# Half of W1's columns by seven block products for eight in a two-layer decoder trunk, with the weight sums made between the steps of the preceding round's W2 product

## The chip, the core and the metric

The kernel runs on one core of a Trainium2 chip. The core has a matrix engine (TensorE, in the profile PE, its weight loads PEld), a vector engine (DVE), a scalar engine (ACT), GpSimd (POOL) and a queue engine that issues the loads (SP). The metric is the device time of one execution in microseconds (us). The kernel before takes 2276.84 us, the median of three runs (2275.48 to 2276.86).

## What is computed

Two layers of a decoder trunk, on 256 rows of 2048 columns in float32. Only the last line of a layer is touched by the change:

```python
x = x + mixed @ w_out[layer]
h2 = _rms(x, norm2_g[layer])
x = x + jnp.square(jax.nn.relu(h2 @ mlp_w1[layer])) @ mlp_w2[layer]
```

W1 is 2048 x 8192, W2 is 8192 x 2048. The four mixers before W_out stay as they are.

## The kernel before, in words

**Precision.** Every large product is made from float32 numbers split into a high and a low part: `x = xh + xl`, `w = wh + wl`, and three products, `xl wh + xh wh + xh wl`, are summed in PSUM. The activations are the stationary operand, transposed to "slots" of two 128-row k tiles by 256 rows (names `Ah`, `Al` for the normed residual, `Bh`, `Bl` for the hidden layer). The weights are the moving operand.

**Weights.** A chunk is two k tiles by 512 columns, 128 x 1024 or 512 KB. `raw` (L138) issues its load on SP's queue into one of four `raw` buffers. `split_chunk` (L147) makes `wh` by a copy on ACT (L153; three buffers) and `wl = raw - wh` by a subtraction on DVE (L154; two buffers). A `raw` buffer is free when both have read it, a `wl` buffer when TensorE has used it.

**A product** (`product`, L157) of 2048 by 512 is eight chunks of 12 matmuls of 128x512: eight on `wh` (L172, L173), then four on `wl` (L177), over two row tiles. It sums into two of four PSUM banks with the tag `mm`; four more banks (tag `ms`) serve the transposes.

**The MLP** (in `run`) goes in four rounds of 2048 hidden columns. In a round, four products of W1, each followed by relu on ACT (L987), the square on DVE (L988), eight transposes and the split into slots `B` (`to_slots`, L195); then four products of W2, each added to the residual `x` on DVE (`residual`, L934). Before it, the last four W_out products each write four transposed k tiles of the residual, times the gain, to slots `A` (`split_slot` with gain, L217 and L218).

**Order.** A scheduler with its own timeline puts each engine's instructions into one fixed order; operations under `hp` (high priority) are placed ahead. On each engine, the instructions then run in that order. SP's loads too.

Of the kernel before, what the change touches and what calls it, by code (L numbers as in the profile page):

```python
# [12 lines left out]
F32 = mybir.dt.float32  # L13
F32R = mybir.dt.float32r
I32 = mybir.dt.int32
AF = mybir.ActivationFunctionType
# [4 lines left out]
P = 128  # L21
# [33 lines left out]
class Trunk:  # L55
# [18 lines left out]
    # ---------------------------------------------------------------- helpers  # L74
# [62 lines left out]
    # ------------------------------------------------------- weights and products  # L137
# [19 lines left out]
    def product(self, chunks, lhs, n=512, before=None):  # L157
        """sum over k of lhs[k]^T @ w[k]; chunks hold two k each. Returns the PSUM tiles of both row tiles."""
# [19 lines left out]
        return acc  # L178
# [16 lines left out]
    def to_slots(self, src, cols, slots, j0, gain=None):  # L195
        """src(t): token-major [128, >=cols] tiles; transposes cols into slot pairs from j0 on."""
        nc = self.nc
        for jj in range(cols // 256):
            pt = self.misc("tp").rearrange("p (k s) -> p k s", k=2)
# [6 lines left out]
            self.split_slot(pt, slots[j0 + jj], gain, 2 * (j0 + jj))  # L206
# [154 lines left out]
    # ---------------------------------------------------------------- norm of the residual  # L361
# [32 lines left out]
    def evac_normed(self, acc, heads, d, r, tag):  # L394
        """token-major copies times r, normed per head"""
# [25 lines left out]
    def head_tr(self, src, dst, engine):  # L421
        """src(t): token-major [128, 4 * 128]; dst [128, 2, 4, 128] (row tile, head, row)"""
# [29 lines left out]
    def s5_table(self, i):  # L452
        """[128, 2, 256]: cos and sin of t * theta for the state column i."""
# [120 lines left out]
    def vones(self, acc, r, name):  # L574
        """values with a column of ones per head: [128, 2, 4, 129]"""
# [50 lines left out]
    # ---------------------------------------------------------------- native sparse attention  # L626
# [8 lines left out]
    def nsa_kv(self, acc, kcol, r, tag):  # L635
        """the key and value column blocks times r, and 128 ** -0.5 times what norms the keys, [128, 2]"""
# [21 lines left out]
    def rope1_tr(self, k, tag):  # L658
        """[128 rows, 128] x 2 -> roped and transposed [128, 256]"""
# [10 lines left out]
    def nsa_compress(self, layer, kcT, vcT):  # L670
        """k_cmp^T [128, 15], its norm scale [15, 1], and [v_cmp | 1] [15, 129]"""
# [5 lines left out]
        for w, xT in enumerate((kcT, vcT)):  # L677
# [6 lines left out]
            # four lags at a time: each column tile sums its own, the rest of its rows stay zero  # L684
# [89 lines left out]
    # ---------------------------------------------------------------- retention  # L774
# [8 lines left out]
    def ret(self, qT, kT, v):  # L783
        """normed retention output, token-major"""
# [150 lines left out]

    def run(self):
# [16 lines left out]
        for layer in range(self.depth):  # L953
# [9 lines left out]
            h2 = self.slots("A")  # L963
            early, late = kt[8:], kt[:8]
            for n in range(4):
                self.residual(self.product([ins["w_out"][layer, 0, n, c] for c in range(4)], early), n)
            for n in range(4):
                self.residual(self.product([ins["w_out"][layer, 1, n, c] for c in range(4)], late), n)
                with self.hp():
                    self.to_slots(lambda t: self.x[t][:, n * 512:], 512, h2, 2 * n, self.gains[:, 1, layer])  # L970
                    self.sumsq(ss, n)
            with self.hp():
                r = self.rstd(ss, "b")
            kt2 = self.ktiles(h2)
# [3 lines left out]
            hT = None  # L978
            for rd in range(4):
                hid = self.slots("B")  # L980
                for n in range(4):
                    acc = self.product([ins["w1"][layer, 4 * rd + n, c] for c in range(8)], kt2)
                    hs = []
                    with self.hp():
                        for t in range(NT):
                            h = self.wk.tile([P, 512], F32, name="hid", tag="rp", bufs=3)
                            nc.scalar.activation(h, acc[t], AF.Relu, scale=r[:, t:t + 1])  # L987
                            V.tensor_tensor(h, h, h, ALU.mult)  # L988
                            hs.append(h)
                        self.to_slots(lambda t: hs[t], 512, hid, 2 * n)  # L990
                kh = self.ktiles(hid)
                if rd == 3 and not last:
                    hT = self.slots("A")
                for n in range(4):
                    acc = self.product([ins["w2"][layer, rd, n, c] for c in range(8)], kh)
                    self.residual(acc, n)
                    if rd == 3:
                        if last:
                            for t in range(NT):
                                nc.scalar.dma_start(self.out[t * P:(t + 1) * P, n * 512:(n + 1) * 512],  # L1000
                                                    self.x[t][:, n * 512:(n + 1) * 512])
                        else:
                            with self.hp():
                                self.to_slots(lambda t: self.x[t][:, n * 512:], 512, hT, 2 * n,
                                              self.gains[:, 0, layer + 1])
                                self.sumsq(ss, n)
# [10 lines left out]
def _chunks(w):  # L1017
    """[K, N] -> [K/256, 128, 2, N]: partition rows of two k tiles side by side"""
# [4 lines left out]
def _layout(i):  # L1023
# [23 lines left out]
    # state columns: partition = (group of the pair, state), column = pair  # L1047
# [44 lines left out]
```

## Time and profile before

| what | value |
|---|---|
| median of three runs | 2276.84 us |
| span of the profiled execution (no other time of it is listed) | 2274.8 us |
| TensorE busy | 2249.3 us (99%) |
| DVE busy | 1411.6 us (62%) |
| ACT busy | 1083.1 us (48%) |
| loaded from memory | 405.61 MB, 179 GB/s over the span |
| granted TensorE clock | 0.999 of full speed |

The profiled execution's span is 2.0 us under the median of the runs. "Busy" of an engine is the time in which one of its instructions ran; matmuls overlap each other in the records (one lasts 0.39 us and the next begins 0.23 us after it), so the count of matmuls in a time says more than their durations. "Idle before" names what ended an engine's idle time. The MLP of layer 0 lies between about 440 and 1135 us from the span's start, that of layer 1 between about 1500 us and the end.

### The profile page before, as it was taken

What the parts mean: (1) busy time and instruction counts of PE and PEld (TensorE: products, weight loads), DVE (VectorE), ACT (ScalarE), POOL (GpSimd) and SP (SyncE); (2) the same over time, 40 slices, a digit from 0 to 9 for tenths busy, and PEclk for the clock granted to TensorE, in tenths of its full rate; (3) what the DMA queues carried; (4) which work ended last, traced back from release to release, by engine and by line L of the source; (5) the groups of instructions that cost most, each with busy time, mean ns of one, the idle gap of its engine ahead of it and who ended that gap; (6) DMA issues with size and microseconds to landing.
All of it is one profiled execution on the core that took longest, in us unless ns stands there. A gap on an engine that the chain in (4) does not pass through costs nothing.

```text
span 2274.8 us, 29209 instructions
## 1 busy us (share of the span) xinstructions
PE 2249.3 (99%) x10732; PEld 1831.1 (80%) x10732; DVE 1411.6 (62%) x2105; ACT 1083.1 (48%) x1410; POOL 144.7 (6%) x396
## 2 busy tenths in 40 slices
PE   8999999999999999999999999999999999999999
PEld 7777778888888888888877777888888888888887
DVE  8988975555555555455569997566554554555554
ACT  6456554544344344344545664445444443443443
POOL 0213111000000000000002212010000000000000
PEclk9999999999999999999999999999999999999999
DMA  7544735555655555555554456355555556556554
GB/s 252 165 133 130 241 113 167 183 182 191 194 185 192 190 192 185 195 186 185 186 175 155 131 152 206 120 178 183 186 192 189 190 181 201 187 190 191 191 194 167
DMA packets 115919, 409.62 MB, mean 180 GB/s; under 512 B 14016, under 2 KB 14272, under 8 KB 115776
## 3 DMA queue, kind: packets, MB, share of 16 engines
q1 hardware_dynamic: 113184, 405.06, 53.8%
q10 hardware_dynamic: 2592, 2.70, 0.3%
q8 instruction: 84, 1.38, 0.2%
q14 instruction: 59, 0.48, 0.1%
HBM read 405.61 MB, written 2.10 MB: 179 GB/s over the span
## 4 chain that ended last, share of the span: by engine, by line
PE 86%; DVE 7%; POOL 3%; issue 2%; ACT 2%; DMA 1%; DVEq 0%; ACTq 0%; SPq 0%
PE mm L177 27%; PE mm L172 27%; PE mm L173 27%; DVE wl L154 2%; PE tp L203 2%; DVE w L515 1%; PE glu L551 1%; POOL rst L89 1%; PE bu L502 1%; PE nsc L759 0%; PE yp L530 0%; PE npv L769 0%; POOL rst L91 0%; POOL rst L90 0%; PE cmp L693 0%
## 5 line engine op out<-in xcount | busy, mean ns | idle before, releaser
L153 ACT ACTIVATE wh<-raw 128x1024 fp32r<-128x1024 f32 (+1 forms) x752 | 790.5, 1052 | 1055.0 <-PE mm L173 944.7
L154 DVE TENSOR_TENSOR wl<-raw,wh 128x1024 fp32r<-128x1024 f32 (+1 forms) x752 | 908.0, 1213 | 594.5 <-PE mm L177 557.6
L172 PE MATMUL mm<-wh,Al 128*128 128x512 f32 (+1 forms) x1728 | 670.1, 389 | 1.9 <-ACT wh L153 1.5
L173 PE MATMUL mm<-wh,Ah 128*128 128x512 f32 (+1 forms) x1728 | 669.1, 388 | 0.0
L172 PE MATMUL mm<-wh,Bl 128*128 128x512 f32 x1280 | 498.4, 389 | 0.9 <-DVE Bl L213 0.9
L173 PE MATMUL mm<-wh,Bh 128*128 128x512 f32 x1280 | 498.4, 389 | 0.0
L177 PE MATMUL mm<-wl,Ah 128*128 128x512 f32 (+1 forms) x1728 | 466.9, 391 | 10.9 <-DVE wl L154 10.5
L177 PEld LDWEIGHTS mm<-wl,Ah 128*128 128x128 f32 x1728 | 316.0, 188 | 88.4 <-DVE wl L154 18.4
L172 PEld LDWEIGHTS mm<-wh,Al 128*128 128x128 f32 x1728 | 325.1, 188 | 73.2 <-issue 4.6
L173 PEld LDWEIGHTS mm<-wh,Ah 128*128 128x128 f32 x1728 | 325.2, 188 | 69.7 <-issue 5.6
L177 PE MATMUL mm<-wl,Bh 128*128 128x512 f32 x1280 | 344.2, 391 | 0.2 <-DVE wl L154 0.2
L172 PEld LDWEIGHTS mm<-wh,Bl 128*128 128x128 f32 x1280 | 240.3, 188 | 51.1 <-DVE Bl L213 1.1
L173 PEld LDWEIGHTS mm<-wh,Bh 128*128 128x128 f32 x1280 | 240.3, 188 | 49.7
L177 PEld LDWEIGHTS mm<-wl,Bh 128*128 128x128 f32 x1280 | 238.6, 188 | 49.0 <-DVE wl L154 0.6
L934 DVE TENSOR_TENSOR x<-mm,x 128x512 f32<-128x512 f32 x96 | 61.8, 686 | 105.5 <-PE mm L177 105.5
L213 DVE TENSOR_TENSOR Bl<-tp,Bh 128x512 fp32r<-128x512 f32 x76 | 52.1, 687 | 70.9 <-ACT Bh L212 70.9
L86 POOL TENSOR_SCALAR rv<-rv 128x2 f32<-128x2 f32 x4 | 1.0, 244 | 879.8 <-DVE rv L372 879.8
L987 ACT ACTIVATE hid<-mm,rb 128x512 f32<-128x512 f32 x64 | 40.6, 685 | 24.2 <-PE mm L177 24.2
L212 ACT ACTIVATE Bh<-tp 128x512 fp32r<-128x512 f32 x76 | 40.8, 584 | 5.7 <-PE tp L203 5.7
L988 DVE TENSOR_TENSOR hid<-hid 128x512 f32<-128x512 f32 x64 | 41.2, 684 | 0.0
L515 DVE TENSOR_TENSOR_SCAN w<-mag,z 128x256 f32<-128x256 f32 x64 | 40.7, 678 | 0.0
L218 DVE SCALAR_TENSOR_TENSOR Al<-tp,gains,Ah 128x256 fp32r<-128x256 f32 x64 | 29.3, 478 | 16.9 <-ACT Ah L217 16.9
(300 smaller groups left out, 1187.4 us busy)
## 6 DMA issues: line engine op xcount, KB each, us to landing
raw<-in_w_dram SPq DMA_DIRECT2D x512, 512.0 KB, 3.4
raw<-in_w_main_dram SPq DMA_DIRECT2D x160, 512.0 KB, 4.0
raw<-in_w_out_dram SPq DMA_DIRECT2D x64, 512.0 KB, 3.6
aux<-in_wcmp_dram SPq DMA_DIRECT2D x16, 512.0 KB, 5.2
raw<-in_w_gate_dram SPq DMA_DIRECT2D x16, 268.0 KB, 2.6
x<-in_x_dram SPq DMA_DIRECT2D x8, 256.0 KB, 5.1
aux<-in_s5g_dram SPq DMA_DIRECT2D x4, 512.0 KB, 4.8
out_dram<-x ACTq DMA_DIRECT2D x8, 256.0 KB, 2.1
```

What stands on the lines that cost most here:

```text
L153: self.nc.scalar.activation(h[:, :cols], r[:, :cols], AF.Copy)
L154: self.nc.vector.tensor_tensor(l[:, :cols], r[:, :cols], h[:, :cols].bitcast(F32), ALU.subtract)
L172: nc.tensor.matmul(acc[t], rows(xl, t), mov(wh, j), start=k == 0, stop=False)
L173: nc.tensor.matmul(acc[t], rows(xh, t), mov(wh, j), start=False, stop=False)
L177: nc.tensor.matmul(acc[t], rows(lhs[k][0], t), mov(wl, j), start=False, stop=k == nk - 1)
L203: nc.tensor.transpose(pt[:, kk, t * P:(t + 1) * P], src(t)[:, c:c + P], self.ident)
L212: nc.scalar.activation(h, pt, AF.Copy)
L213: nc.vector.tensor_tensor(l, pt, h.bitcast(F32), ALU.subtract)
L515: V.tensor_tensor_scan(w[:, c, :], mg, z[:, c, :], 0.0, ALU.mult, ALU.add)
L934: self.nc.vector.tensor_tensor(x, acc[t], x, ALU.add)
L987: nc.scalar.activation(h, acc[t], AF.Relu, scale=r[:, t:t + 1])
L988: V.tensor_tensor(h, h, h, ALU.mult)
```

## The change

Two neighbouring column blocks of W1 (512 columns each, blocks 0 and 1 of a round) and the two row tiles and the two k tiles of a chunk form a 2 x 2 by 2 x 2 block product. The kernel before makes it by eight block products; the change makes it by seven (a Strassen-Winograd scheme), each again by three matmuls (`three`). Blocks 2 and 3 of a round are made as before (`plain`). For each chunk the seven are: two with unchanged operands (`first_steps`, banks p1, p2), and five with sums of blocks (`sums_steps`, banks p3 to p7).

- `sums_slot`: the sums of activation blocks, made once per layer when the slots `A` are written, with their own split (`Sh`, `Sl`).
- `sums_steps`: per chunk it loads both W1 blocks (block 0 a second time), makes four differences on DVE (L251 to L254; `t13`, `t24`), splits three operands on ACT (L262) and DVE (L263), and issues 15 matmuls.
- `pair_first`, `pair_last`: combine p1 to p7 to the four results; relu and square are now both on ACT (`act2`).
- `mlp`: in rounds 1 to 3 one sums step is put after every fourth chunk of the preceding round's W2 product (`second`); in round 0 after every second chunk of the two plain W1 products. The W2 product of the last round comes alone.

```diff
+    def sums_slot(self, pt, slot, gain, k):
...
+        a = self.wk.tile([P, 2, SEQ], F32, name="ga", tag="w")
+        for kk in range(2):
+            nc.scalar.activation(a[:, kk, :], pt[:, kk, :], AF.Copy, scale=gain[:, k + kk:k + kk + 1])
+        nc.scalar.activation(h, a, AF.Copy)
+        V.tensor_tensor(l, a, h.bitcast(F32), ALU.subtract)
...
+        V.tensor_tensor(s[:, 0, :], blk(1, 0), blk(1, 1), ALU.add)
+        V.tensor_tensor(s[:, 1, :], s[:, 0, :], blk(0, 0), ALU.subtract)
+        V.tensor_tensor(s[:, 2, :], blk(0, 0), blk(1, 0), ALU.subtract)
+        V.tensor_tensor(s[:, 3, :], blk(0, 1), s[:, 1, :], ALU.subtract)
...
+        nc.scalar.activation(sh, s, AF.Copy)
+        V.tensor_tensor(sl, s, sh.bitcast(F32), ALU.subtract)
...
+    def three(self, acc, x, w, first, last):
+        nc = self.nc
+        (xh, xl), (wh, wl) = x, w
+        nc.tensor.matmul(acc, xl, wh, start=first, stop=False)
+        nc.tensor.matmul(acc, xh, wh, start=False, stop=False)
+        nc.tensor.matmul(acc, xh, wl, start=False, stop=last)
...
+        for c, src in enumerate(chunks):
+            w = self.split_chunk(src)
+            for kk in range(2):
+                self.three(acc[kk], [x[:, kk, :P] for x in slots[c]], [y[:, kk * 512:(kk + 1) * 512] for y in w],
+                           c == 0, c == last)
...
+                b1 = self.raw(chunks1[c]).rearrange("p (k n) -> p k n", k=2)
+                b2 = self.raw(chunks2[c]).rearrange("p (k n) -> p k n", k=2)
+                ta, tb = (self.wk.tile([P, 2, 512], F32, name=nm, tag="aux", bufs=2) for nm in ("t13", "t24"))
+                V.tensor_tensor(ta[:, 0, :], b2[:, 0, :], b1[:, 0, :], ALU.subtract)
+                V.tensor_tensor(ta[:, 1, :], b2[:, 1, :], b2[:, 0, :], ALU.subtract)
+                V.tensor_tensor(tb[:, 0, :], b2[:, 1, :], ta[:, 0, :], ALU.subtract)
+                V.tensor_tensor(tb[:, 1, :], tb[:, 0, :], b1[:, 1, :], ALU.subtract)
...
+                ah = self.wp.tile([P, 1024], F32R, name="t13h", tag="wh", bufs=3)
+                al = self.wp.tile([P, 1024], F32R, name="t13l", tag="wl", bufs=2)
...
+                for h, l, x in ((bh, bl, b2[:, 1, :]), (ah, al, f2(ta)), (dh, dl, f2(tb))):
+                    nc.scalar.activation(h, x, AF.Copy)
+                    V.tensor_tensor(l, x, h.bitcast(F32), ALU.subtract)
...
+            self.three(acc[3], S(3), (bh, bl), *f)
+            self.three(acc[5], S(0), half((ah, al), 0), *f)
+            self.three(acc[7], S(2), half((ah, al), 1), *f)
+            self.three(acc[6], S(1), half((dh, dl), 0), *f)
+            self.three(acc[4], [x[:, 1, P:] for x in slots[c]], half((dh, dl), 1), *f)
...
+            if rd:
+                mix(second(rd - 1, hid), ys, 4, 1)
+                hid = self.slots("B")
+            else:
+                hid = self.slots("B")
+                mix(both(plain(rd, n, hid) for n in (2, 3)), ys, 2, 1)
+            done = pair_last(p, v1, c11)
...
-            for rd in range(4):
-                hid = self.slots("B")
-                for n in range(4):
-                    acc = self.product([ins["w1"][layer, 4 * rd + n, c] for c in range(8)], kt2)
```

**The order on DVE in a W2 product.** In the kernel before, DVE's rows of the W2 products of a round are (`x` the residual, `wl` the low parts of the weights):

```order
L934 TENSOR_TENSOR x_78<-mm_5031,x_78 128x512
L934 TENSOR_TENSOR x_79<-mm_5032,x_79 128x512
L154 TENSOR_TENSOR wl<-raw,wh 128x1024 x8
L934 TENSOR_TENSOR x_78<-mm_5179,x_78 128x512
L934 TENSOR_TENSOR x_79<-mm_5180,x_79 128x512
L154 TENSOR_TENSOR wl<-raw,wh 128x1024 x8
```

In the changed kernel, the rows of the second group of four chunks of such a product, with the step at the product's end (`t13l`, `t24l`, `bl` are low parts of the sums and of one block):

```order
L154 TENSOR_TENSOR wl<-raw,wh 128x1024 x2
L251 TENSOR_TENSOR t_6988<-raw 128x512
L252 TENSOR_TENSOR t_6988<-raw 128x512
L263 TENSOR_TENSOR bl<-raw,bh 128x512
L253 TENSOR_TENSOR t_6989<-raw,t_6988 128x512
L1033 TENSOR_TENSOR x_78<-mm_6719,x_78 128x512
L1033 TENSOR_TENSOR x_79<-mm_6720,x_79 128x512
L154 TENSOR_TENSOR wl<-raw,wh 128x1024
L254 TENSOR_TENSOR t_6989<-t_6989,raw 128x512
L263 TENSOR_TENSOR t13l<-t_6988,t13h 128x1024
L263 TENSOR_TENSOR t24l<-t_6989,t24h 128x1024
```

The two L251/L252 rows read two `raw` buffers and stand behind the split of the product's last chunk and of the next one's first; the two additions to `x` stand behind four of the step's rows.

**The order on DVE at the start of the MLP.** Before, from the last W_out product's addition to `x` on:

```order
L934 TENSOR_TENSOR x_78<-mm_4234,x_78 128x512
L934 TENSOR_TENSOR x_79<-mm_4235,x_79 128x512
L154 TENSOR_TENSOR wl<-raw,wh 128x1024 x2
L372 TENSOR_REDUCE rv<-ss 128x2
L218 SCALAR_TENSOR_TENSOR Al_3633<-tp,gains,Ah_3632 128x256
L154 TENSOR_TENSOR wl<-raw,wh 128x1024
L218 SCALAR_TENSOR_TENSOR Al_3635<-tp,gains,Ah_3634 128x256
```

and in the changed kernel (`ga`, `gs` the activations and their block sums, `Sl` the sums' low parts):

```order
L1033 TENSOR_TENSOR x_78<-mm_4294,x_78 128x512
L215 TENSOR_TENSOR Sl<-gs,Sh 128x512
L1033 TENSOR_TENSOR x_79<-mm_4295,x_79 128x512
L154 TENSOR_TENSOR wl<-raw,wh 128x1024 x2
L215 TENSOR_TENSOR Sl<-gs,Sh 128x512
L471 TENSOR_REDUCE rv<-ss 128x2
L209 TENSOR_TENSOR gs<-ga 128x128
L207 TENSOR_TENSOR gs<-ga 128x128
L154 TENSOR_TENSOR wl<-raw,wh 128x1024
L207 TENSOR_TENSOR gs<-ga 128x128
L209 TENSOR_TENSOR gs<-ga 128x128
L154 TENSOR_TENSOR wl<-raw,wh 128x1024
```

Each `wl` row there now has rows of the sums between it and the next.

## Rows read from the trace of the kernel before

**Rows 1.** The page, parts 1, 2 and 4: busy time, clock, chain that ended last.

```profile
PE 2249.3 (99%) x10732; PEld 1831.1 (80%) x10732; DVE 1411.6 (62%) x2105; ACT 1083.1 (48%) x1410; POOL 144.7 (6%) x396
...
PE 86%; DVE 7%; POOL 3%; issue 2%; ACT 2%; DMA 1%; DVEq 0%; ACTq 0%; SPq 0%
```

**Rows 2.** Stretches: us, length, busy (count) per engine, clock, DMA share, GB/s.

```profile
core 0: us, PE busy (x) PEld busy (x) DVE busy (x) ACT busy (x) POOL busy (x), PEclk, DMA share, GB/s
...
600.00:700.00 100.00, 100.00 (x455) 83.08 (x454) 51.20 (x50) 44.58 (x48) 0.00 (x0) 1.00 0.57 189
...
1200.00:1300.00 100.00, 96.34 (x492) 74.11 (x491) 92.73 (x174) 60.17 (x89) 21.89 (x45) 1.00 0.47 145
```

**Rows 3.** DVE's timeline in a W2 product: start, duration, idle time before.

```profile
599.05 1.23 DVE L154 TENSOR_TENSOR wl<-raw,wh 128x1024 fp32r<-128x1024 f32 x1 [1.50 <-PE mm L177]
601.77 1.22 DVE L154 TENSOR_TENSOR wl<-raw,wh 128x1024 fp32r<-128x1024 f32 x1 [1.49 <-PE mm L177]
604.49 1.23 DVE L154 TENSOR_TENSOR wl<-raw,wh 128x1024 fp32r<-128x1024 f32 x1 [1.50 <-PE mm L177]
...
610.78 1.29 DVE L934 TENSOR_TENSOR x<-mm,x 128x512 f32<-128x512 f32 x2 [2.35 <-PE mm L177]
611.98 2.35 DVE L154 TENSOR_TENSOR wl<-raw,wh 128x1024 fp32r<-128x1024 f32 x2
```

**Rows 4.** Groups by shape: busy us, mean ns of one, idle before.

```profile
L154 DVE TENSOR_TENSOR wl<-raw,wh 128x1024 fp32r<-128x1024 f32 x736 | 896.4, 1223 | 593.6 <-PE mm L177 556.7 <-issue 29.0 <-ACT np L761 4.4
...
L988 DVE TENSOR_TENSOR hid<-hid 128x512 f32<-128x512 f32 x64 | 41.2, 684 | 0.0
...
L388 DVE TENSOR_TENSOR k1r<-ko,rc 128x128 f32<-128x128 f32 x8 | 2.2, 278 | 0.0
```

**Rows 5.** The same view for ACT.

```profile
L153 ACT ACTIVATE wh<-raw 128x1024 fp32r<-128x1024 f32 x736 | 780.1, 1060 | 1045.2 <-PE mm L173 938.6 <-DVE wl L154 29.4 <-DMA raw<-in_w_main_dram 19.3
L212 ACT ACTIVATE Bh<-tp 128x512 fp32r<-128x512 f32 x76 | 40.8, 584 | 5.7 <-PE tp L203 5.7
```

**Rows 6.** Waits of TensorE, 0 to 440 us, costliest: total us, times, longest.

```profile
PE mm L177 <- DVE wl L154: 4.2, 7, 1.8
```

**Rows 7.** SP's own waits: total us, times, longest.

```profile
SPq L140 <- DVE wl L154: 1806.7, 700, 11.5
```

**Rows 8.** The tile raw, 500 to 1000 us: loads, and their time to landing.

```profile
L140 SPq DMA_DIRECT2D raw<-in_w_dram x180: 327/328/328, 501.7 to 997.7; - x180
...
DMA to landing us min/median/max: 3.0/3.4/5.7
```

**Rows 9.** The tile raw, 0 to 30 us, where loads crowd.

```profile
L140 SPq DMA_DIRECT2D raw<-in_w_main_dram x11: 327/328/559, 1.7 to 29.1; - x11
...
DMA to landing us min/median/max: 3.7/5.6/8.8
```

**Rows 10.** The page, part 2: GB/s in the first slices of 57 us.

```profile
GB/s 252 165 133 130 241 113 167 183 182 191 194 185 192 190 192 185 195 186 185 186 175 155 131 152 206 120 178 183 186 192 189 190 181 201 187 190 191 191 194 167
```

**Rows 11.** TensorE's timeline, transposes of a hidden tile, 461 us.

```profile
461.04 1.04 PE L203 MATMUL tp<-ident,hid 128*128 128x128 f32 x8
...
461.83 1.17 PE L177 MATMUL mm<-wl,Ah 128*128 128x512 f32 x4
```

More of the change, by code (lines that the diff above doesn't have):

```diff
@@ L157, in product, with product_steps @@
     def product(self, chunks, lhs, n=512, before=None):
+        acc = []
+        for _ in self.product_steps(acc, chunks, lhs, n, before):
+            pass
+        return acc
+    def product_steps(self, out, chunks, lhs, n=512, before=None):
         nc = self.nc
@@ new lines, in three, with first_steps @@
+    def three(self, acc, x, w, first, last):
+        nc = self.nc
+        (xh, xl), (wh, wl) = x, w
+        nc.tensor.matmul(acc, xl, wh, start=first, stop=False)
+        nc.tensor.matmul(acc, xh, wh, start=False, stop=False)
+        nc.tensor.matmul(acc, xh, wl, start=False, stop=last)
+    def first_steps(self, out, chunks, slots):
+        acc = [self.ps.tile([P, 512], F32, name=f"p{i}", tag="mm") for i in (1, 2)]
+        last = len(chunks) - 1
+        for c, src in enumerate(chunks):
[3 more added lines that the diff above has]
+                           c == 0, c == last)
+            if c == last:
+                out.extend(acc)
+            yield
@@ L193, in ktiles, with to_slots @@
         return [(slots[k // 2][0][:, k % 2, :], slots[k // 2][1][:, k % 2, :]) for k in range(KT)]
-    def to_slots(self, src, cols, slots, j0, gain=None):
+    def to_slots(self, src, cols, slots, j0, gain=None, sums=None, bank=None):
         nc = self.nc
         for jj in range(cols // 256):
-            pt = self.misc("tp").rearrange("p (k s) -> p k s", k=2)
+            pt = (bank or self.misc)("tp").rearrange("p (k s) -> p k s", k=2)
             for kk in range(2):
@@ L205, in to_slots @@
                 slots[j0 + jj] = self.slot("B", j0 + jj)
-            self.split_slot(pt, slots[j0 + jj], gain, 2 * (j0 + jj))
+            if sums is not None:
+                sums.append(self.sums_slot(pt, slots[j0 + jj], gain, 2 * (j0 + jj)))
+            else:
+                self.split_slot(pt, slots[j0 + jj], gain, 2 * (j0 + jj))
     def split_slot(self, pt, slot, gain=None, k=0):
@@ L934, in residual, with act2, mlp, mix @@
                 self.nc.vector.tensor_tensor(x, acc[t], x, ALU.add)
+    def act2(self, c, x, r, t):
+        S = self.nc.scalar
+        S.activation(c, x, AF.Relu, scale=r[:, t:t + 1])
+        S.activation(c, c, AF.Square)
+    def mlp(self, layer, h2, sums, r, ss, last):
+        nc = self.nc
+        V = nc.vector
+        kt2 = self.ktiles(h2)
+        w1 = lambda rd, n: [self.ins["w1"][layer, 4 * rd + n, c] for c in range(8)]
+        bank = lambda name: self.ps.tile([P, 512], F32, name=name, tag="mm")
+        tmp = lambda nm, tag, n: self.wk.tile([P, 512], F32, name=nm, tag=tag, bufs=n)
+        nxt = [None]
+        def mix(xs, ys, every, off):
+            for i, _ in enumerate(xs):
+                if i % every == off:
+                    next(ys, None)
+            for _ in ys:
+                pass
+        def pair_first(rd):
+            p = []
+            for _ in self.first_steps(p, w1(rd, 0), h2):
+                pass
+            with self.hp():
+                v1, c11 = tmp("v1", "ev", 4), tmp("c11", "ev", 4)
+                nc.scalar.activation(v1, p[0], AF.Copy)
+                V.tensor_tensor(c11, p[1], v1, ALU.add)
+                self.act2(c11, c11, r, 0)
+            return v1, c11
+        def pair_last(p, v, c11):
+            with self.hp():
+                c12, c21, c22 = (tmp(nm, "rp", 3) for nm in ("c12", "c21", "c22"))
+                V.tensor_tensor(v, p[6], v, ALU.add)
+                V.tensor_tensor(c12, p[3], v, ALU.add)
+                V.tensor_tensor(v, p[7], v, ALU.add)
+                V.tensor_tensor(c12, p[5], c12, ALU.add)
+                self.act2(c12, c12, r, 0)
+                V.tensor_tensor(c22, p[5], v, ALU.add)
+                self.act2(c22, c22, r, 1)
+                V.tensor_tensor(c21, v, p[4], ALU.subtract)
+                self.act2(c21, c21, r, 1)
+            return (c11, c21), (c12, c22)
+        def plain(rd, n, hid):
+            acc = []
+            yield from self.product_steps(acc, w1(rd, n), kt2)
+            with self.hp():
+                hs = []
+                for t in range(NT):
+                    hs.append(tmp("hid", "ev", 4))
+                    self.act2(hs[t], acc[t], r, t)
+                self.to_slots(lambda t: hs[t], 512, hid, 2 * n, bank=bank)
+        def second(rd, hid):
+            kh = self.ktiles(hid)
+            for n in range(4):
+                acc = []
+                yield from self.product_steps(acc, [self.ins["w2"][layer, rd, n, c] for c in range(8)], kh)
+                self.residual(acc, n)
+                if rd == 3:
+                    if last:
+                        for t in range(NT):
+                            nc.scalar.dma_start(self.out[t * P:(t + 1) * P, n * 512:(n + 1) * 512],
+                                                self.x[t][:, n * 512:(n + 1) * 512])
+                    else:
+                        with self.hp():
+                            self.to_slots(lambda t: self.x[t][:, n * 512:], 512, nxt[0], 2 * n,
+                                          self.gains[:, 0, layer + 1])
+                            self.sumsq(ss, n)
+        def both(gens):
+            for g in gens:
+                yield from g
+        hid = None
+        for rd in range(4):
+            v1, c11 = pair_first(rd)
+            p = {}
+            ys = self.sums_steps(p, w1(rd, 0), w1(rd, 1), h2, sums)
+            if rd:
+                mix(second(rd - 1, hid), ys, 4, 1)
+                hid = self.slots("B")
+            else:
+                hid = self.slots("B")
+                mix(both(plain(rd, n, hid) for n in (2, 3)), ys, 2, 1)
+            done = pair_last(p, v1, c11)
+            with self.hp():
+                for n in range(2):
+                    self.to_slots(lambda t: done[n][t], 512, hid, 2 * n)
+            if rd:
+                for _ in both(plain(rd, n, hid) for n in (2, 3)):
+                    pass
+        if not last:
+            nxt[0] = self.slots("A")
+        for _ in second(3, hid):
+            pass
+        return nxt[0]
@@ L963, in run @@
             h2 = self.slots("A")
+            sums = []
             early, late = kt[8:], kt[:8]
@@ L969, in run @@
                 with self.hp():
-                    self.to_slots(lambda t: self.x[t][:, n * 512:], 512, h2, 2 * n, self.gains[:, 1, layer])
+                    self.to_slots(lambda t: self.x[t][:, n * 512:], 512, h2, 2 * n, self.gains[:, 1, layer], sums)
                     self.sumsq(ss, n)
@@ L973, in run @@
                 r = self.rstd(ss, "b")
-            kt2 = self.ktiles(h2)
             last = layer == self.depth - 1
@@ L977, in run @@
                 ss = self.sm.tile([P, NT, 4], F32, name="ss", tag="ss", bufs=2)
-            hT = None
-            for rd in range(4):
-                hid = self.slots("B")
-                for n in range(4):
-                    acc = self.product([ins["w1"][layer, 4 * rd + n, c] for c in range(8)], kt2)
[L983 to L1006, printed above, removed]
+            hT = self.mlp(layer, h2, sums, r, ss, last)
             if not last:
```

31 lines of the change are left out of this document (30 added, 1 removed).

## The prediction

> **What bounds the kernel now.** I read the page first: TensorE is busy for 99% of the span, and it holds 86% of the chain that ended last [rows 1]. Then the table of stretches: inside the MLP TensorE is busy for all of a 100 us stretch, at full granted clock, DVE for half of it and ACT for less [rows 2]. DVE's timeline shows why: it splits one weight chunk per 2.72 us and idles 1.5 us before each, ended by TensorE's release of the `wl` buffer [rows 3]. So DVE, ACT and the loads wait for TensorE, not the reverse. The longest wait of TensorE for DVE in the first 440 us is 1.8 us, and all such waits there total 4.2 us [rows 6]. SP idles 1807 us for DVE's release of a `raw` buffer [rows 7]: loads are issued only as buffers come free, four at a time in all. Where TensorE is busy for 96% of a stretch, the granted clock is still 1.00 [rows 2]; short waits have no price through the clock here.
>
> A measurement of this kernel can tell about 0.2%, 4.6 us, from no change.
>
> **What is removed.** A block pair took 192 matmuls of 128x512 and takes 168. Four pairs per layer, two layers: 192 fewer; in the written order the products of this size go from 8832 to 8640, so the change does what it says. Twelve matmuls take 2.72 us by the starts [rows 3], 0.2265 us each: 192 x 0.2265 = **43.5 us**, all on TensorE's path. The Trainium skill, "TensorE: Matmul & The Clock Gate", section "Back-to-back issue gap", has N/2.4 + 2.5 ns, 216 ns for 512 columns; by it the gain would be 41.4 us. The trace has 226.5 ns, and it decides.
>
> **What is added, and what hides it.** The squares move from DVE to ACT (64 of 0.68 us [rows 4]); ACT has the room, so 0. Per layer 32 W1 chunks are loaded twice, 33.5 MB in all; on top of 405.6 MB nothing, as long as the rate stays below what the kernel already reaches, 252 GB/s in its first slice [rows 10].
>
> *W2 with sums, rounds 1 to 3.* A group is four chunks and one sums step: 4 x 12 + 15 = 63 matmuls, 14.3 us. DVE back to back needs 1.18 us for a 1024 tile and 0.645 for a 512 tile by its pairs [rows 3]. It has four splits (4.7), four differences and one small split (3.2), two large ones (2.4), and half of two additions to `x` (0.65): 10.9 us, 76%. ACT: 6 x 1.06 + 0.58 [rows 5] = 6.9 us. Loads: six chunks, 3.15 MB, 220 GB/s. On average all fits. What can fail is order. I followed one W2 product (two groups) instruction by instruction, engine by engine. The step at the product's end has least room: its second W1 block lands in the `raw` buffer that the split of the product's last chunk frees, and that split waits until TensorE has used the preceding step's `t13l`. From there: release 0.2, split 1.22, landing 3.4 [rows 8], two differences 1.33, ACT's split 1.06, four hand-offs at about 0.05: 7.4 us. TensorE meanwhile has 35 matmuls, 7.93 us. So 0.53 us is left, and it is gone at a landing of 3.93 us. The landing is 3.4 at 190 GB/s [rows 2, 8] and 5.6 where loads crowd at the start [rows 9]; 220 GB/s is nearest to the first, so I take 4.2: 0.3 us lost at each of 24 such places (four per round, three rounds, two layers): **7.2 us**. Bounds: 0, and 1.67 x 24 = 40.
>
> *Start of the MLP.* From the last addition of W_out to the first sums step DVE has nine splits (10.6), nine 512 tiles (5.8), eight 128x128 sums of about 0.25 (0.278 alone [rows 4]) and a reduction: 18.6 us. TensorE has 68 matmuls and eight transposes of 0.1 us [rows 11]: 16.2 us; in this stretch a chunk feeds only six matmuls, 1.36 us against 1.18 on DVE, so there is no room to catch up. The difference is 2.4; walking the rows in order, with `wl` rows queued behind sums, TensorE waits 4.6 us. Twice: **9.2 us** (bounds 4.8 and 12).
>
> *Round 0, plain W1 with sums.* A period of two chunks and a step: 39 matmuls, 8.83 us; DVE 2 x 1.18 + 5 x 0.645 + 2 x 1.18 = 7.9. It fits, but where a hidden tile is finished, relu, square and transposes queue behind the step's work on ACT: 0.7 each layer, **1.4 us**.
>
> *Round 0 to round 1.* The six additions of `pair_last` (4 us), six slot splits (3.9) and ten chunk splits (11.8) stand in one stretch of DVE, 19.7 us, against 68 matmuls and 32 transposes, 18.6 us, and bank p4 is free only after the sixth addition. Walked: 3.0 us, twice: **6 us** (bounds 2 and 8).
>
> *Last W_out products.* DVE per product 4.7 + 1.3 + 4.6 for the block sums = 10.6 us against TensorE's 11.7: 1 us a layer for order, **2 us** (bounds 0 and 6). *Later hand-overs* (`pair_last` beside plain chunks of 2.72 us, DVE with two splits of lead): 0.5 us, six times, **3 us**.
>
> Lost: 7.2 + 9.2 + 1.4 + 6 + 2 + 3 = 28.8. Sum: 43.5 - 28.8 = 14.7 us. The span would go from 2274.8 to 2260.1; the runs stand 2.0 above the span, so from their median, 2276.84, I forecast **2262.1 us**, 0.65% faster.
>
> **Rivals.**
>
> *The four raw buffers become the bound (slower).* A sums step holds two of them at once, so a longer landing goes straight into the chain above. For: the chain has 0.53 us to spare, and landings reach 5.7 us in the MLP even now [rows 8]. Against: the median there is 3.4, and the demand rises by only a sixth. Each us of landing above 3.93 costs 24 us; with the other losses (21.6) the gain is used up at 4.84, and the kernel is slower by more than 4.6 us from 5.03 on. At 5.6, the crowded median [rows 9], it loses 40: 43.5 - 21.6 - 40 = -18, **2295 us**. The Trainium skill, "DMA: Bandwidth & Descriptors", section "Latency and other measured facts", gives memory access 0.2 us on average and 2 us at high load; by that rule a landing of 3.4 could become an estimated 5.2, 24 x 1.27 = 30 lost there, some 2285 us. No stretch here runs 220 GB/s of chunk loads alone, so the trace neither bears it out nor excludes it. Chance 0.15.
>
> *TensorE stays the bound nearly everywhere (much faster).* DVE's lead of two `wl` buffers covers the order, landings stay at 3.4, and only the start of the MLP (4.8) and round 0 to 1 (2) cost: 43.5 - 6.8 = 36.7, **2240 us**. For: DVE is at 76% in three rounds of four. Against: in round 0 its work and TensorE's are within a few per cent of each other. Chance 0.2.
>
> *DVE becomes the bound in round 0 (no change).* The step's differences depend on one another, and DVE runs its rows in order. If latencies and hand-offs make a period of 7.9 us one of 9.5, TensorE waits 0.7 us in each of 16 periods: 11 us more, **2273 us**. For: 90% load, and a mixer stretch in which DVE is at 93% leaves TensorE idle 3.7 us in 100 [rows 2]. Against: rows that follow each other there overlap by 0.05 us, they don't gap [rows 3]. Chance 0.13.
>
> **How the numbers follow.** Forecast 0.52, rivals 0.15, 0.2, 0.13. Faster by over 0.2% (below 2272.3): the forecast nearly whole, 0.48, and the second rival: 0.68. Within 0.2%: the rest of the forecast and the third rival: 0.17. Slower: the first rival, 0.15. Faster cases hold most of the chance; by themselves they lie between 2240 and 2272. The range for 8 in 10: at the low end all losses at their lower bounds but for hand-overs, near 2243; at the high end the raw buffers at a landing near 5.2, 2286.
>
> **What would show it.** Right: the W1 and W2 stretches hold the same matmuls per us as before except at the start of the MLP and after round 0's last step, where TensorE idles for `wl` and slot splits, 3 to 6 us each; waits at L221 and L222 for ACT's split of `t13` and `bh`, some tenths each, at products' ends; landing of `raw` 3.6 to 4.4; DVE near 75% in rounds 1 to 3 and over 90% in round 0. Wrong: TensorE waiting in every group of W2 for `t13h` or for a load (first rival), in every period of round 0 (third), or nowhere beyond a us (second). The gain itself would be wrong if a matmul of the new products took other than 0.2265 us, or if the granted clock fell below 1.00 in the MLP.

## The result, and the profile after

The changed kernel takes 2343.57 us (median of four runs, 2340.26 to 2347.64) against 2276.85 for the kernel before in the same comparison: 1.0292 times as long, with a 95% interval of 1.0278 to 1.0307. The forecast was 2262.1, with a range of 2243 to 2286. The profiled execution has a span of 2338.5 us, 63.7 more than before, although TensorE has 43.5 us less to do: 107 us went into losses that the kernel before doesn't have.

The page of the changed kernel, parts 1, 4 and 6 (the last row's final number is the median time to landing):

```profile
PE 2259.8 (97%) x10540; PEld 1800.8 (77%) x10540; DVE 1690.3 (72%) x2545; ACT 1229.7 (53%) x1640; POOL 161.8 (7%) x396
...
PE 68%; DVE 11%; DMA 10%; ACT 6%; issue 3%; POOL 3%; DVEq 0%; ACTq 0%; SPq 0%
PE mm L179 18%; PE mm L180 18%; PE mm L184 17%; DMA raw<-in_w_dram 9%; DVE wl L154 4%; PE p L221 3%; PE p L223 3%; PE p L222 3%; ACT wh L153 2%; PE tp L299 2%; ACT t13h L262 1%; ACT hid L1038 1%; DVE t L251 1%; PE bu L601 1%; DVE t L252 1%
...
raw<-in_w_dram SPq DMA_DIRECT2D x576, 512.0 KB, 4.1
```

Against [rows 1], TensorE's share of the chain fell from 86% to 68%, and loads of `raw` now hold 9% of it. TensorE's busy time rose by 10.5 us where 43.5 us of matmuls were taken away: a matmul's record lasts 0.39 us where the next begins 0.23 us after it, so a stall of a tenth or two, or a matmul at half clock, hides inside "busy". So I also read the starts: for each stretch of the program, its length less its matmuls of 128x512 at 0.2265 us each and its transposes (a few records are missing, and where one stretch ends and the next begins moves some us between neighbours, so a figure may be some us off).

| where | predicted loss, us | by the starts, both layers |
|---|---|---|
| start of the MLP, to the first sums step | 9.2 | 12.1 |
| round 0 | 1.4 | 19.7 |
| round 0 to round 1 | 6 | 8.1 |
| W2 with sums, rounds 1 to 3 | 7.2 | 26.2 |
| plain W1 products, rounds 1 to 3 | not in the sum | 34.1 |
| p1 and p2, rounds 2 and 3 (hand-overs) | 3 | 4.6 |
| last W_out products | 2 | under 1 |
| sum | 28.8 | 105 |

The waits of TensorE over the whole span (total us, times, longest) name the costliest place:

```profile
PE tp L299 <- ACT hid L1039: 30.0, 15, 3.4
PE mm L184 <- DVE wl L154: 11.3, 15, 1.8
PE mm L179 <- ACT wh L153: 5.5, 8, 2.3
PE p L221 <- ACT t24h L262: 5.3, 5, 2.3
```

TensorE's timeline shows it, at a step of round 0, at the end of a plain product of round 1, and at a step of round 3 (start, duration; in brackets the idle time before and what ended it):

```profile
482.54 0.63 PE L223 MATMUL p<-t13l,Sh 128*128 128x512 f32 x2
485.03 0.50 PE L221 MATMUL p<-t24h,Sl 128*128 128x512 f32 x1 [1.86 <-ACT t24h L262]
485.36 0.40 PE L222 MATMUL p<-t24h,Sh 128*128 128x512 f32 x1
...
688.16 1.07 PE L184 MATMUL mm<-wl,Ah 128*128 128x512 f32 x4
691.19 0.44 PE L299 MATMUL tp<-ident,hid 128*128 128x128 f32 x2 [1.96 <-ACT hid L1039]
691.38 0.48 PE L179 MATMUL mm<-wh,Al 128*128 128x512 f32 x1
...
692.37 0.63 PE L180 MATMUL mm<-wh,Ah 128*128 128x512 f32 x1
692.80 0.63 PE L179 MATMUL mm<-wh,Al 128*128 128x512 f32 x1
...
944.77 0.50 PE L221 MATMUL p<-bh,Sl 128*128 128x512 f32 x1 [0.84 <-ACT bh L262]
945.10 0.40 PE L222 MATMUL p<-bh,Sh 128*128 128x512 f32 x1
946.11 0.50 PE L223 MATMUL p<-bl,Sh 128*128 128x512 f32 x1 [0.61 <-DVE bl L263]
946.68 0.50 PE L221 MATMUL p<-t13h,Sl 128*128 128x512 f32 x1
947.01 0.39 PE L222 MATMUL p<-t13h,Sh 128*128 128x512 f32 x1
```

The last four `wl` matmuls of the product begin at 688.16; the transposes of its own result come right behind, and wait. ACT's timeline there shows for what:

```profile
688.41 1.06 ACT L153 ACTIVATE wh<-raw 128x1024 fp32r<-128x1024 f32 x1 [1.71 <-PE mm L180]
689.37 1.25 ACT L1038 ACTIVATE hid<-mm,rb 128x512 f32<-128x512 f32 x2
690.51 1.14 ACT L1039 ACTIVATE hid<-hid 128x512 f32<-128x512 f32 x2
```

Relu and square take 2.3 us, and until the first has read a bank no further product can sum there. And the wait has an echo: from 691.95 on matmuls start 0.43 us apart. The stretches give the granted clock (length, busy and count per engine, clock, DMA share, GB/s):

```profile
680.00:688.00 8.00, 8.00 (x43) 6.78 (x42) 5.86 (x7) 4.19 (x6) 0.00 (x0) 1.00 0.50 177
688.00:691.40 3.40, 1.44 (x9) 0.90 (x7) 1.22 (x1) 2.99 (x5) 0.00 (x0) 1.00 0.40 154
691.40:696.00 4.60, 4.60 (x15) 3.64 (x14) 0.00 (x0) 1.31 (x2) 0.00 (x0) 0.63 0.32 116
696.00:700.00 4.00, 4.00 (x22) 3.33 (x22) 1.74 (x2) 2.03 (x3) 0.00 (x0) 1.00 0.37 129
```

A wait of 1.96 us, then 4.6 us with a mean clock of 0.63, most of it at the lower level of 1.2 GHz. It doesn't follow every wait: of the twelve such waits in rounds 1 to 3, five had it behind them (behind the same wait at 873 us the matmuls keep their 0.23). By the starts, 87 matmuls of this size stood 0.40 to 0.45 us apart, 10 before: some 15 us.

Last, the loads, 440 to 1040 us: ACT's waits for a load of `raw`, and the landing of the tile `raw` (before: [rows 8]).

```profile
ACT bh L262 <- DMA raw<-in_w_dram: 89.4, 31, 5.2
...
ACT wh L153 <- DMA raw<-in_w_dram: 59.7, 64, 2.7
```

```profile
DMA to landing us min/median/max: 3.0/4.1/6.1
```

The landing is what the prediction took, 4.1 for 4.2. Yet ACT waits for a load 95 times in this stretch. In the kernel before it waited once:

```profile
ACT wh L153 <- DMA raw<-in_w_dram: 2.0, 1, 2.0
```

### The profile page after: what moved, and what is told of

It reads as the page before. It is cut to its first block, busy times and chain, and to the rows that moved or that the text cites. A ratio compares the mean times of both kernels' runs of the same rounds, so it can differ in the third digit from the quotient of the medians.

```text
span 2338.5 us, 29470 instructions
## 1 busy us (share of the span) xinstructions
PE 2259.8 (97%) x10540; PEld 1800.8 (77%) x10540; DVE 1690.3 (72%) x2545; ACT 1229.7 (53%) x1640; POOL 161.8 (7%) x396
## 4 chain that ended last, share of the span: by engine, by line
PE 68%; DVE 11%; DMA 10%; ACT 6%; issue 3%; POOL 3%; DVEq 0%; ACTq 0%; SPq 0%
PE mm L179 18%; PE mm L180 18%; PE mm L184 17%; DMA raw<-in_w_dram 9%; DVE wl L154 4%; PE p L221 3%; PE p L223 3%; PE p L222 3%; ACT wh L153 2%; PE tp L299 2%; ACT t13h L262 1%; ACT hid L1038 1%; DVE t L251 1%; PE bu L601 1%; DVE t L252 1%
## 5 line engine op out<-in xcount | busy, mean ns | idle before, releaser
L153 ACT ACTIVATE wh<-raw 128x1024 fp32r<-128x1024 f32 (+1 forms) x688 | 720.5, 1049 | 733.7 <-PE mm L180 478.8
L154 DVE TENSOR_TENSOR wl<-raw,wh 128x1024 fp32r<-128x1024 f32 (+1 forms) x688 | 830.5, 1211 | 380.3 <-PE mm L184 279.5
L179 PE MATMUL mm<-wh,Al 128*128 128x512 f32 (+1 forms) x1216 | 477.6, 394 | 5.6 <-ACT wh L153 3.6
L180 PE MATMUL mm<-wh,Ah 128*128 128x512 f32 (+1 forms) x1216 | 475.0, 392 | 0.0
L184 PE MATMUL mm<-wl,Ah 128*128 128x512 f32 (+1 forms) x1216 | 334.8, 395 | 11.4 <-DVE wl L154 11.1
L184 PEld LDWEIGHTS mm<-wl,Ah 128*128 128x128 f32 x1216 | 223.3, 190 | 72.3 <-DVE wl L154 19.7
L179 PEld LDWEIGHTS mm<-wh,Al 128*128 128x128 f32 x1216 | 231.5, 190 | 59.5 <-ACT wh L153 8.5
L180 PEld LDWEIGHTS mm<-wh,Ah 128*128 128x128 f32 x1216 | 231.8, 191 | 50.3 <-issue 5.6
L262 ACT ACTIVATE bh<-raw 128x512 fp32r<-128x512 f32 x64 | 40.5, 633 | 181.9 <-DMA raw<-in_w_dram 181.9
L251 DVE TENSOR_TENSOR t<-raw 128x512 f32<-128x512 f32 x64 | 44.2, 691 | 94.0 <-DMA raw<-in_w_dram 94.0
L262 ACT ACTIVATE t13h<-t 128x1024 fp32r<-128x1024 f32 x64 | 67.8, 1060 | 47.6 <-DVE t L252 43.1
L263 DVE TENSOR_TENSOR t24l<-t,t24h 128x1024 fp32r<-128x1024 f32 x64 | 78.4, 1224 | 19.5 <-ACT t24h L262 19.1
L263 DVE TENSOR_TENSOR t13l<-t,t13h 128x1024 fp32r<-128x1024 f32 x64 | 77.9, 1218 | 0.2
L262 ACT ACTIVATE t24h<-t 128x1024 fp32r<-128x1024 f32 x64 | 67.0, 1047 | 5.5 <-DVE t L254 5.5
```

The costliest lines, as they stand in the source:

```text
L153: self.nc.scalar.activation(h[:, :cols], r[:, :cols], AF.Copy)
L154: self.nc.vector.tensor_tensor(l[:, :cols], r[:, :cols], h[:, :cols].bitcast(F32), ALU.subtract)
L179: nc.tensor.matmul(acc[t], rows(xl, t), mov(wh, j), start=k == 0, stop=False)
L180: nc.tensor.matmul(acc[t], rows(xh, t), mov(wh, j), start=False, stop=False)
L184: nc.tensor.matmul(acc[t], rows(lhs[k][0], t), mov(wl, j), start=False, stop=k == nk - 1)
L251: V.tensor_tensor(ta[:, 0, :], b2[:, 0, :], b1[:, 0, :], ALU.subtract)
```

## The experiments

Two theories came out of this. **Banks:** in the plain products the transposes were moved into the four `mm` banks, so the product, its transposes and the next product don't fit side by side. **Raw ring:** the steps' loads wait for four `raw` buffers that the chunks also use. Rivals: the squares in ACT's queue, the order of the rows on DVE and ACT, the rate of the loads.

**1. Other banks for the transposes of rounds 1 to 3.**

```diff
-                self.to_slots(lambda t: hs[t], 512, hid, 2 * n, bank=bank)
+                self.to_slots(lambda t: hs[t], 512, hid, 2 * n, bank=None if rd else bank)
```

> Only the PSUM banks of the transposes in the plain W1 products of rounds 1 to 3 change: from the four banks that the products sum in to the four others, as in the kernel before. Theory (banks): the two row tiles of the finished product and its two transposed tiles fill all four banks, so the next product can start only after ACT's relu has emptied the first ones, and the order puts the transposes right there; TensorE waits 1.9 to 2.0 us at each of 12 ends of such a product, and runs at half clock for some 3 us after some of them. Then the waits for ACT's hid in these rounds are gone (only those of round 0 are left), and the time falls from 2343.6 by 26 to 36 us, to 2308 to 2318. Rival (squares): ACT's queue, with the squares on it, is what is late; then the wait only moves to another row and the time falls by under 8 us. Rival (four raw buffers): under 5 us.

Measured: 2319.82 us, 23.8 less than the changed kernel (1.0182 times before, 1.0167 to 1.0198). TensorE's timeline at the end of the same product, then its waits:

```profile
690.94 1.07 PE L184 MATMUL mm<-wl,Ah 128*128 128x512 f32 x4
691.84 0.39 PE L180 MATMUL mm<-wh,Ah 128*128 128x512 f32 x1
692.07 0.39 PE L179 MATMUL mm<-wh,Al 128*128 128x512 f32 x1
...
697.97 0.38 PE L299 MATMUL tp<-ident,hid 128*128 128x128 f32 x2
```

```profile
PE tp L299 <- ACT hid L1039: 8.1, 3, 3.9
```

The next product (from 691.84 on) follows the old one without a wait, the transposes come 6 us later, and only three waits are left, in round 0 and at its end. That is the theory, a little under its size. It shows that the banks made the order and the wait; the squares alone can't, since they are still on ACT.

**2 and 3. The squares back on DVE**, alone and with the other banks.

```diff
-        S.activation(c, c, AF.Square)
+        self.nc.vector.tensor_tensor(c, c, c, ALU.mult)
```

> Only the squares go back from ACT to DVE, for all results of W1. Theory (banks): the transposes still stand right behind the finished product, and DVE has a weight split of 1.22 us in front of the squares; the waits of TensorE for hid stay between 1.5 and 2.5 us each, the time changes by under 8 us either way. Rival (squares): the wait of 1.96 us at each product's end falls by the two squares, 1.1 us, at 16 places, with what the clock costs after them: 15 to 25 us less. Rival (four raw buffers): no change, under 5 us.

> Both edits. Theory (banks): what the other banks give alone, within 6 us; DVE gets some 45 us more work in stretches where it is not the bound. Rival (squares): the sum of two gains, at least 10 us below the run with the banks alone.

Measured: 2365.45 us alone, 21.9 more than the changed kernel; 2330.26 with the banks, 10.4 more than these alone. With the squares on DVE the wait stays (this row is of the run with the squares alone):

```profile
PE tp L299 <- DVE hid L1039: 26.1, 14, 2.1
```

Both of my numbers were too small: I had said under 8 and within 6 us. DVE is the scarcer engine here. So the rival falls, and moving the squares to ACT was right.

**4. Round 0 as before**, with the other banks throughout.

```diff
+            if rd == 0:
+                hid = self.slots("B")
+                for n in range(4):
+                    for _ in plain(0, n, hid):
+                        pass
+                continue
             v1, c11 = pair_first(rd)
```

> Round 0 of each MLP as in the kernel before (four plain W1 products, 8688 matmuls of 128x512 for 8640), with the transposes of all plain products in the other four banks; the block sums of the activations are still made for rounds 1 to 3. Theory (banks): round 0 with its sums lost 11 to 14 us per layer against its matmuls, because p3 to p7 leave the plain products only three banks of eight; with it plain that goes, and so do the 3.5 us of the passage to round 1, for 5.4 us of matmuls: 8 to 13 us per layer better than the run with the banks of rounds 1 to 3 alone, 2285 to 2300. Rival (DVE is the bound wherever a sums step runs): 11 to 14 us saved for 5.4, so 12 to 17 in all, but the other rounds keep their losses too. Rival (four raw buffers): round 0 had 266 GB/s in its densest part; plain again, its landings fall, and the gain is of the same size, but the landings of rounds 1 to 3 stay above 4 us and so do their losses.

Measured: 2292.09 us (1.0061, 1.0046 to 1.0076), 27.7 below the first run, with 48 matmuls (10.9 us) more to do. Round 0 and its passages thus cost 38.6 us (27.7 + 10.9), 3.5 times the 10.9 that its seven products save. By the starts the 48 steps of the other rounds still lose 23 us.

**5 and 6. Two buffers more for the steps' loads, or no second load of block 0**, both on run 4.

```diff
-                b1 = self.raw(chunks1[c]).rearrange("p (k n) -> p k n", k=2)
+                b1 = self.wk.tile([P, 2, 512], F32, name="b1", tag=("Tk", "vones")[c % 2], bufs=1)
+                nc.sync.dma_start(b1, chunks1[c].rearrange("p (k n) -> p k n", k=2))
...
-                dh = self.wk.tile([P, 1024], F32R, name="t24h", tag=("Tq", "Tk")[c % 2], bufs=1)
-                dl = self.wk.tile([P, 1024], F32R, name="t24l", tag=("s5b", "vones")[c % 2], bufs=1)
+                dh = self.wk.tile([P, 1024], F32R, name="t24h", tag="Tq", bufs=1)
+                dl = self.wk.tile([P, 1024], F32R, name="t24l", tag="s5b", bufs=1)
```

```diff
-                b1 = self.raw(chunks1[c]).rearrange("p (k n) -> p k n", k=2)
                 b2 = self.raw(chunks2[c]).rearrange("p (k n) -> p k n", k=2)
+                b1 = b2
```

> As the run with round 0 plain (2292.1 us), but in the sums steps block 0 is loaded into two buffers of its own (space that the mixers use and the MLP doesn't), so the four raw buffers are shared by five loads of a group for six; the parts of t24 get one buffer in place of two. Theory (raw ring): at a product's last step the load of the step's blocks waits for raw buffers that are still being split, and the chain load, differences, splits then ends after TensorE's other matmuls; the waits and short stalls at the 48 steps, 23 us in that run by the starts of the matmuls, fall to under 8, and the time to 2272 to 2280. Rival (order on DVE and ACT): the step's rows stand behind splits of other chunks in any case; the time changes by under 5 us. Rival (rate of the loads): the loads as such are what is slow at 220 GB/s; under 5 us, with landings still above 4 us.

> As the run with round 0 plain, but block 0 is not loaded a second time: the differences read block 1 in its place (left out: 48 loads of 512 KB and block 0 in the differences; no instruction on DVE, ACT or TensorE is left out). Theory (raw ring): the same gain as with two more buffers, to within 5 us, 2270 to 2282. Rival (rate of the loads): clearly more than two more buffers give, 2270 or less where those stay near 2290. Rival (order on DVE and ACT): under 5 us.

Measured: 2267.91 and 2267.03 us. Two more buffers, and a sixth fewer loads in these rounds, give the same, 24 to 25 us, so it is the buffers and not the rate. The rival of the order on DVE and ACT, under 5 us, falls too. The losses at the 48 steps fell from 23 to 6 us. And 2267.91 beats both kernels: 0.9962 times before, 0.9950 to 0.9975. Its page, parts 1 and 4:

```profile
PE 2237.4 (99%) x10588; PEld 1801.0 (79%) x10588; DVE 1613.1 (71%) x2435; ACT 1210.3 (53%) x1606; POOL 151.6 (7%) x396
...
PE 82%; DVE 8%; DMA 3%; POOL 3%; issue 2%; ACT 2%; DVEq 0%; ACTq 0%; SPq 0%
```

**7. The whole change with both repairs** (the edits of runs 1 and 5).

> The whole change with the transposes of rounds 1 to 3 in the other four banks (2319.8 us) and block 0 in two buffers of its own. Theory (raw ring): 14 to 26 us less, and in round 0 the waits for the hid tiles and the weight splits stay: 2294 to 2306. Rival (order, or the single t24 buffer in round 0's short periods): under 8 us.

Measured: 2285.46 us (2279.17 to 2290.91; 1.0035, 1.0020 to 1.0050), 34.4 below run 1. The landing and ACT's waits, 440 to 1040 us:

```profile
DMA to landing us min/median/max: 3.1/4.2/6.2
```

```profile
ACT bh L262 <- DMA raw<-in_w_dram: 39.1, 25, 3.1
...
ACT wh L153 <- DMA raw<-in_w_dram: 14.7, 21, 1.4
```

The loads land no faster, but ACT waits for them 54 us in place of 149: they are issued earlier. I had expected less, and waits for hid in round 0; the trace of this run has none left, though the transposes of round 0 still lie in the `mm` banks. Against run 5, round 0 with its sums still costs 28.5 us (17.6 + 10.9) for the 10.9 that it saves. By the starts, both layers, 10.5 us go before the first sums step, 9.4 in round 0 and 9.0 in the passage to round 1. TensorE's timeline at its start and end, the rows with over 0.2 us of idle time:

```profile
435.25 0.72 PE L223 MATMUL p<-wl,Ah 128*128 128x512 f32 x2 [0.26 <-DVE wl L154]
438.59 0.72 PE L223 MATMUL p<-wl,Ah 128*128 128x512 f32 x2 [0.32 <-DVE wl L154]
442.88 0.74 PE L223 MATMUL p<-wl,Ah 128*128 128x512 f32 x2 [1.07 <-DVE wl L154]
445.52 0.50 PE L179 MATMUL mm<-wh,Al 128*128 128x512 f32 x1 [0.99 <-ACT wh L153]
...
523.66 0.33 PE L299 MATMUL tp<-ident,c 128*128 128x128 f32 x1 [0.99 <-DVE v L1073]
527.91 0.50 PE L221 MATMUL p<-wh,Al 128*128 128x512 f32 x1 [1.06 <-DVE c L1080]
539.47 0.50 PE L179 MATMUL mm<-wh,Bl 128*128 128x512 f32 x1 [2.26 <-ACT wh L153]
```

**8. The two buffers alone**, on the changed kernel.

> The changed kernel with nothing but block 0 of the sums steps in two buffers of its own (the transposes stay in the accumulators' banks, round 0 stays). Theory (two separate causes): the raw ring alone is worth what it is worth beside the other banks, 34 us, to within 8: 2302 to 2318, with the waits for hid unchanged. Rival (the losses cover each other: a wait of 2 us at a product's end lets the loads catch up): clearly less, 2320 to 2340.

Measured: 2320.70 us, 22.9 less, where beside the other banks it was 34.4. I had expected 2302 to 2318; it lies at the near edge of the rival's range. So the losses cover each other in part, by some 11 us. Part of that is the clock: in the profiled executions its mean rose from 0.991 to 0.993 with the buffers alone and from 0.995 to 1.000 beside the other banks, some 5 and 11 us of the span. That late loads catch up while TensorE waits at a product's end would be the rest; no run shows it. The waits for hid:

```profile
PE tp L299 <- ACT hid L1039: 23.0, 12, 2.0
```

Twelve are left, two for each of six rounds; the three of round 0 went with the ring, though its transposes stayed in the `mm` banks.

**9. Round 0's sums in two banks in place of five**, on run 7, its transposes in the banks that come free.

```diff
-        acc = {i: self.pm.tile([P, 512], F32, name=f"p{i}", tag="ms") for i in (6, 7, 5, 3)}
-        acc[4] = self.ps.tile([P, 512], F32, name="p4", tag="mm")
+        acc = {i: self.pm.tile([P, 512], F32, name=f"p{i}", tag="ms") for i in ((7, 5) if few else (6, 7, 5, 3))}
+        acc.update({3: acc[5], 6: acc[7], 4: acc[7]} if few else {4: self.ps.tile([P, 512], F32, name="p4", tag="mm")})
```

> As the run with the whole change, the other banks and the two buffers (2285.5 us), but in round 0 the five sums of the steps are added up in two PSUM banks in place of five (left out: round 0's results of these products are not kept apart), and the transposes of round 0 go to the two that come free; no instruction less. Theory (banks): what round 0 loses there it loses because the next plain product and the transposes have no free bank; then the waits for hid are gone in round 0 too, and the time falls by 10 to 20 us, to 2265 to 2275. Rival (DVE, with 90% of round 0's time, and the passages at its start and end): under 6 us, 2280 to 2287.

Measured: 2281.39 us (1.0021, 1.0011 to 1.0031), 4 below run 7 with intervals that overlap. My theory, 10 to 20 us, falls. By the starts round 0 itself lost 3.5 us in this run, both layers, where it was 9.4 in run 7; 12.2 stand before the first sums step and 9.7 in the passage to round 1. So of the rival the passages are what stands; DVE as the bound inside round 0 doesn't show.

**10 and 11. Two tries to go on from run 5**: p1 and p2 between the chunks of the preceding plain product, and two of their eight chunks in the two buffers.

```diff
+            box = []
+            ps = pair_first(rd + 1, box) if rd < 3 else iter(())
+            next(ps, None)
+            mix(plain(rd, 3, hid), ps, 1, 0)
```

```diff
-            w = self.split_chunk(src)
+            w = self.split_chunk(src, own={3: "Tk", 6: "vones"}.get(c))
```

> As the run with round 0 plain and the two buffers, but the first products p1 and p2 of a round are put chunk by chunk between those of the preceding round's last plain product. Alone they ask for a chunk of 512 KB per six matmuls, 1.36 us, which is 385 GB/s; among plain chunks it is two per 18 matmuls, 4.1 us, 257 GB/s. Theory (the loads bound p1 and p2): the 2 to 2.5 us that each round loses there go, 6 to 14 us over six rounds below the run without it. Rival (banks: p1 and p2 beside the plain product fill the four banks, and the next W2 product waits for their emptying): no gain, or up to 8 us slower.

> As the run with round 0 plain and block 0 in two buffers of its own (2267.9 us), but the fourth and the seventh chunk of p1 and p2 of a round are loaded into these two buffers as well. Theory (p1 and p2 are short of loads: six matmuls, 1.36 us, per 512 KB): two of eight chunks are there early, and of the 2 us that each of six rounds loses there a half goes: 4 to 8 us less, 2260 to 2264. Rival (in p1 and p2 the splits on DVE and ACT, 1.2 us of 1.36, end last): within 3 us of 2267.9.

Measured: 2271.93 us, 4.0 slower than run 5 (0.9978, 0.9969 to 0.9987), and 2266.93, no different from it (0.9957, 0.9944 to 0.9970). Loads aren't what p1 and p2 lack; whether the first failed for want of banks was not tried.

## Why the prediction was wrong

**What held.** 192 matmuls fewer, at 0.2265 us. The landing (4.2 taken, 4.1 seen). The start of the MLP: 9.2 predicted, 12.1 by the starts, with the waits for `wl` named. The passage to round 1: 6 against 8.1. The squares on ACT, put at 0: on DVE they cost 10 to 22 us more (runs 2 and 3).

**The step that failed first: a hand-over left out of the sum.** For rounds 1 to 3 I costed the W2 products, and under "later hand-overs" only `pair_last`; the end of a plain product was costed in round 0 alone. The diff gives its transposes `bank`, a tile of the four `mm` banks. Two banks for the product, two for its transposes: none for the next product until relu is done. Before, the transposes lay in the `ms` banks, and a product began while the last one was being emptied. This cost 23.8 us (run 1). No rival of mine had it.

**The second: "0.3 us lost at each of 24 such places".** The place was right: in rounds 1 to 3 the steps lost some 20 us by the starts, five sixths of it at these 24, so some 0.7 each. The waits for `bl` were mostly 0.3 us, as I had it. But the rows at 946 us show what comes with a wait. `L221` begins 0.57 us after the one before, because it waits once more, 0.07 us for ACT's `t13h`, too short for the view to mark. The matmul behind a waiting one begins 0.33 us after it, not 0.23, as it does at 485.36. And 0.16 us of every wait hide behind a record of 0.39 us. So a wait costs its idle time and some 0.27 us more, however short it is, and a step can have two or three. And round 0, for which I allowed 0.7 a layer, has the same ring with a step every 8.8 us: at the ends of its two plain products per layer it lost 3 to 4.5 us each, 15 of its 19.7 us by the starts. With the two buffers alone (run 8) round 0 lost 9.7, with the other banks of rounds 1 to 3 alone (run 1) 21.1. Altogether the ring cost 22.9 us on the changed kernel and 34.4 with the banks repaired, against 7.2. My first rival had the cause and the sign, but its condition was wrong: it wanted a landing of 5.03, and 4.1 was enough. The Trainium skill, "Perfetto Trace Analysis", section "Optimization Strategy", says that the same gap repeating on the engine that should be saturated can mean too little SBUF or PSUM for the next tile; both gaps here are that, by runs 1, 5 and 6.

**The third: "short waits have no price through the clock here".** The stretches of [rows 2] showed waits that cost nothing; they were shorter or elsewhere. The trace of the kernel before had one that did, and it is the 1.8 us of [rows 6] (TensorE's timeline, then the stretch behind it):

```profile
88.00 1.21 PE L177 MATMUL mm<-wl,Ah 128*128 128x512 f32 x4 [1.85 <-DVE wl L154]
```

```profile
89.30:92.70 3.40, 3.40 (x11) 2.62 (x10) 3.40 (x8) 0.97 (x3) 0.00 (x0) 0.51 0.77 251
```

A wait of 1.85 us, then 3.4 us at 0.51. In the changed kernel a wait of 1.96 us was followed by a clock of 0.63 for 4.6 us, and the mean clock of the profiled execution is 0.991 for 0.999 before: 15 us by the starts, some 19 by the mean over the span, where the sum had nothing. With both repairs it is 1.000 again (run 7).

**The third rival**, DVE as the bound in round 0, is not borne out as it stood. With banks and ring repaired, and with more banks still (run 9), the change as a whole is not faster than before; without round 0 it is. But the rival wanted a wait in each of 16 periods, and round 0 itself loses 3.5 us in run 9; what is left stands before its first step and behind its last, 19.5 us in run 7 and 21.9 in run 9, where the prediction had 15.2. TensorE waits there for rows of DVE and ACT (`wl`, `wh`, `v`, `c`); whether their number or their order makes them late was not tried.

So even repaired, the whole change loses 52 us (2276.85 - 43.5 = 2233.4 against 2285.5), not 28.8.

## What to carry to other kernels

Count the buffers of every shared pool through the whole period, PSUM banks and landing buffers alike, at the places where one piece of work hands over to the next: an average of 76% on the second engine says nothing of them. A tile moved to another pool in passing is a change of its own, to be costed with what can no longer overlap. A transformation that saves 2% of a bound engine's work pays only if nothing else on that engine's path gets a wait, and the stage with the least slack (here round 0) is best left as it is.

## What was not expected of the hardware

A wait costs more than its idle time: the matmul behind the waiting one began 0.33 us after it in place of 0.23 (485.03 and 485.36, 946.68 and 947.01), and 0.16 us of the wait itself don't show as idle, some 0.27 us in all, whether the idle time was 0.07 us or 1.86. And one idle stretch of 1.96 us was enough, in some places but not in others that look alike, for the granted clock to fall afterwards: it was 1.00 before and 0.63 on the mean over the next 4.6 us. The loads landed little later than before: in 4.1 to 4.3 us (medians, 440 to 1040 us) in the six changed kernels read for it, at 211 to 218 GB/s over that time, with four buffers or six, where at 190 GB/s it had been 3.4.
